# Small-K matmuls padded to 128 rows, and per-token factors spread by transposes of a repeated column

## The chip, the cores and the metric

The kernel runs on one core of a Trainium2 chip. The metric is the device time of one execution in microseconds, as the median of several runs; lower is better. A profile of one execution gives the rows that are quoted below. In it PE is TensorE (matmuls), PEld its weight loads, DVE VectorE, ACT ScalarE, POOL GpSimd and SP the engine that issues the transfers.

## The reference, cut to what matters

Two transformer blocks over 512 tokens of 1024 features, in float32. The first has neighbourhood attention (8 heads of 64 features, each query against 256 keys of its window and 256 context keys) beside a Hyena mixer with long convolutions, and a SwiGLU. The second has latent attention (8 heads of 96 features), a state-space branch, cross attention, and a convolutional feed-forward.

```python
def rmsnorm(x, g):
    y = xf * lax.rsqrt(jnp.mean(xf * xf, axis=-1, keepdims=True) + RMS_EPS)
...
    s_nb = jnp.einsum('brqhd,brikhd->bhrqik', grid(q_rot), k_band,
                      preferred_element_type=jnp.float32) * scale + bias[None]
    s_ctx = jnp.einsum('brqhd,bchd->bhrqc', grid(q), k_ctx, preferred_element_type=jnp.float32) * scale
    s = jnp.concatenate([s_nb.reshape(B, H, R, GRID_W, wh * GRID_W), s_ctx], axis=-1)
    p = jax.nn.softmax(s, axis=-1).astype(v.dtype)
...
    h = (hid @ w3.astype(f32)).reshape(L, 2, HY_ORDER, HY_WIDTH)
```

Three things of it matter here: the scores of the neighbourhood attention (a product over 64 features), the last product of the network that makes Hyena's filters (also over 64), and the factors that go with a token: one over the root mean square in every norm, and one over the softmax's sum in every attention.

## The kernel before, in words

Activations lie with features on the 128 partitions and tokens along the free axis. A float32 product is carried by three matmuls on 12-bit parts: a value is split into a high and a low part, and hi times hi, hi times lo and lo times hi are added in one bank of PSUM. A product over 64 features is packed into two matmuls: the queries' high and low parts stand on 64 partitions each and meet the keys' high parts, which stand there twice (128 rows); then the queries' high parts alone meet the keys' low parts, which takes 64 rows (`scores`, with the operands from `stacked_queries` and `stacked_keys`; the low parts of both heads share one tile). `filters` does the same with the filter network's hidden values. In `mla` the keys and queries of a head fill 96 rows.

A factor by token comes out of a sum with the tokens on the partitions, [128 tokens, n], and is needed along the free axis, the same on every partition. `to_rows` splits it into high and low parts (a copy on ACT, a subtraction on DVE), transposes both on PE into 2n rows, and copies them back to SBUF on ACT. Then `spread` (called by `bcast` for the norms) or `over_sums` (for the softmax's sums) makes each block of 128 tokens with a matmul of 4, 8 or 16 rows against a table of zeros and ones (`onehot`, `pick`).

The program is first traced into a list of calls. A planner (`Trace.schedule`, run forwards and backwards by `plan`) then orders the calls of each engine with a table of durations, hands out the memory (96 pages of 512 columns, 8 banks of PSUM), and `emit` issues them in the order of their planned starts. So every instruction of the profile has the line of `emit`, L690, and tiles are named after their pool: `pages` and `small` are SBUF, `banks` is PSUM. Each engine takes its instructions in that fixed order. Generators mix the work: the neighbourhood attention (two pairs of heads to a page, four query blocks to a head) is interleaved with Hyena's branch of the merge, the state-space branch with cross attention and the projections of the gates.

Of the kernel before, what the change touches and what calls it, by code (L numbers as in the profile page):

```python
"""Two transformer blocks on one core: a modulated block (neighbourhood attention beside a Hyena
mixer, SwiGLU) and a hybrid block (latent attention, S5, cross attention, convolutional GLU).

Activations lie with features on partitions and tokens on the free axis. A float32 product is
carried by three passes of 12-bit parts: x = hi + lo exactly, and hi*hi + hi*lo + lo*hi.
In the first block the tokens are ordered by column block, row, column within the block, so that
an attention window is a run of neighbouring tokens.
"""
# [16 lines left out]
P = 128  # L25
D = 1024
T = 512
# [5 lines left out]
SHARE = 0.5, 0.5  # of the memory kept back: for all else, for rounded operands  # L33
RESERVE = 4, 40, 0.05  # units kept back from calls ahead of others: at least, at most, by call
# [14 lines left out]
# columns of the packed per-feature vectors: name -> (first column, columns)  # L49
# [21 lines left out]
# ---------------------------------------------------------------- layout on the host  # L71
def _cols(v):
    """[n] -> [128, n/128], features on partitions (short vectors padded with zeros)."""
    v = np.asarray(v).reshape(-1)
    n = -(-v.size // P)
    w = np.zeros(n * P, v.dtype)
    w[: v.size] = v
    return w.reshape(n, P).T


def _blocks(w):
    """[K, M] -> groups of eight 128x128 blocks, ordered by output tile, then by input tile."""
    k, m = w.shape
    b = w.reshape(k // P, P, m // P, P).transpose(2, 0, 1, 3).reshape(-1, P, P)
    return np.ascontiguousarray(b.reshape(-1, 8, P, P).transpose(0, 2, 1, 3)).reshape(-1, P, 8 * P)


def _rows(w):
    """[1024, 512] -> groups of two input tiles, side by side"""
    return w.reshape(KT // 2, 2, P, T).transpose(0, 2, 1, 3).reshape(KT // 2, P, 2 * T)  # L90


def _token_perm():
    """perm[t'] = t for the token order of the first block."""
    t = np.arange(T)
    cb, r, c = t // 64, (t % 64) // 8, t % 8
    return r * 64 + cb * 8 + c


def _state_order():  # L100
    """the state-space branch's features by half of the group pairs, group of the pair, pair, channel"""
# [7 lines left out]
def _rpb_index():  # L109
    """Index into [na_rpb of a head | NEG] of every (query, key) of a window; three kinds of window."""  # L110
# [14 lines left out]
def _constants():  # L125
# [31 lines left out]
    c["onehot"] = np.repeat(np.eye(8, dtype=f), 2, 0)  # L157
    one = np.repeat(np.eye(8, dtype=f), 2, 0)
    c["pick"] = np.concatenate([np.repeat(one[:, :4], P, 1), np.repeat(np.stack([one[:, :4], one[:, 4:]], 2).reshape(16, 8), 64, 1)], 1)
# [5 lines left out]
def layout(inp):  # L165
# [4 lines left out]
    ones = lambda v: np.concatenate([v[:64], np.ones(32, v.dtype)])  # the rotated part has its gain in the tables  # L170
# [39 lines left out]
    # second block  # L210
# [17 lines left out]
    kvb = f1("w_kv_b_2").reshape(2, P, 2, 4, 2, 64)  # k, p, half, head, (key, value), dim  # L228
# [14 lines left out]
# ---------------------------------------------------------------- tracing  # L243
# The program is traced into a list of calls first. A list scheduler then orders the calls by the
# engines' rates and hands out the on-chip memory as pieces come and go, and they are emitted in that order.
ENGINES = ("tensor", "vector", "scalar", "gpsimd", "sync")
PE, DVE, ACT, POOL, DMA = range(5)
# ns from the end of a call to the start of one that waits for it, by their engines
# [7 lines left out]
ALONE = (DVE,)  # engines that urgent calls have to themselves  # L256
DMA_START = 1700.0
RELEASE = 200.0, 150.0, 150.0, 100.0, 1200.0
TABLES = {AF.Silu: (0,), AF.Sin: (1, 0), AF.Exp: (2,), AF.Gelu_apprx_tanh: (3,)}  # sets of functions of ACT
TABLE_LOAD = 1283.0  # L260
TICK, TICK_COLUMNS = 10240 / 3, 3060.0  # PE's clock is halved after a tick (ns) with fewer columns of 128 rows


class Piece:
    """a piece of an arena, or (arena None) memory that stays"""
# [7 lines left out]
    def box(self, ap):  # L273
        """the partitions and columns that a view may touch"""
# [14 lines left out]
    def access(self, number, box, write):  # L289
        """note an access; returns the calls that it must follow"""  # L290
# [11 lines left out]
class View:  # L302
    """an access pattern that knows its piece of memory"""
# [15 lines left out]
    def placed(self):  # L319
        """the access pattern where the piece has come to lie"""  # L320
# [16 lines left out]
class Arena:  # L337
    """memory in units of `unit` columns, in segments that each hold either rounded operands or
    anything else; the run of units that has been free for longest goes first"""
# [8 lines left out]
    def reset(self, counted):  # L348
        """for another schedule; `counted`: units are only counted"""
        self.counted = counted  # L350
        self.free = self.low = self.n
        self.room = [self.n, self.n]  # units for either kind
# [32 lines left out]
    def take(self, piece, ahead):  # L385
        """place a piece that goes `ahead` of the calls before it, if the memory left allows"""
# [62 lines left out]
class Engine:  # L449
    """an engine whose calls are traced"""  # L450
# [12 lines left out]
class Trace:  # L463
# [8 lines left out]
    def first(self):  # L472
        """calls that go before all others"""
# [5 lines left out]
    def time(engine, name, out, args, kw):  # L479
        """about how long a call holds its engine, in ns"""  # L480
# [17 lines left out]
    def may_swap(engines, name, kw):  # L498
        """whether either of DVE and GpSimd may take a call"""
# [38 lines left out]
    def schedule(self, order, back=False):  # L538
        """Start times and memory for all calls, by a list scheduler that goes by `order`; returns the time it
        takes. back: from the end to the start, on the engines chosen before."""  # L540
# [126 lines left out]
    def plan(self):  # L667
        """Schedules to and fro: each goes by the order that the one before it ended up with."""
# [24 lines left out]
# ---------------------------------------------------------------- the program  # L693
class Program:
# [16 lines left out]
    # tiles  # L711
# [13 lines left out]
    def pair(self, n=T):  # L725
        """a hi/lo pair [128, n]"""
# [8 lines left out]
    def kept(self, pool, shape, name):  # L735
        """memory that stays"""
# [16 lines left out]
    # hi/lo parts  # L753
    def lo(self, out, src, hi, pool=None):
        """out = src - hi"""
# [8 lines left out]
    def mm(self, out, w, x, start, stop):  # L764
        """out (+)= w^T x for hi/lo pairs"""
# [7 lines left out]
    def stream(self, ap):  # L773
        """the 128x128 blocks of a weight in order, as hi/lo pairs"""
# [8 lines left out]
    def proj(self, blocks, xs, n=T, tag="mm"):  # L783
        """one output tile: sum over the input tiles"""
# [5 lines left out]
    def proj_rows(self, ap, xs):  # L790
        """a projection to 512 features with the 256 tokens on partitions: two tiles in PSUM"""
# [45 lines left out]
    def when(self, name):  # L837
        """hold a filler until what it needs has been emitted"""
# [19 lines left out]
    def sincos(self, ang):  # L858
        """ang [parts, n], reduced in place; returns (sin, cos)"""
# [11 lines left out]
    def exp(self, x, n):  # L871
        """e^x for a few columns [128, n], to the last places; in place"""
# [1448 lines left out]
```

## Time and profile before

| | us |
|---|---|
| median of 3 runs | 1847.07 |
| lowest and highest of them | 1846.66 and 1848.56 |
| span of the profiled execution, from first to last instruction | 1843.7 |

The span is 3.4 us shorter than the median of the runs, which also hold what lies before the first and after the last instruction. The page of the profile has PE busy for 96% of the span, DVE for 66%, ACT for 40% and POOL for 20%. A matmul's record is longer than the step to the next one, since matmuls are pipelined; what a matmul costs PE is read from the length of a run of equal ones.

### The profile page before, as it was taken

The page shows a single profiled execution, that of the slowest core. Times are in us where ns is not written, and L with a number is a line of the kernel's source. Part 1 is how long each engine was busy: PE and PEld are TensorE (multiplying, and loading weights), DVE is VectorE, ACT ScalarE, POOL GpSimd, SP SyncE. Part 2 cuts the span into 40 slices and gives each one's busy share as a digit, 9 for nine tenths or more (in the row PEclk, how much of TensorE's full clock was granted, in tenths as well). Part 3 has the DMA queues.
Part 4 walks back from the last instruction along what each step waited for, and adds up shares of the span by engine and source line. Part 5 has one row for each costly group of instructions (what it writes and reads, how often), then busy time and mean ns, then how long its engine had stood idle before and what let it go on. Part 6 is the DMA issues. An engine that isn't in the chain of part 4 may idle for free. (4 is left out here: it accounts for less than half of the span.)

```text
span 1843.7 us, 23257 instructions
## 1 busy us (share of the span) xinstructions
PE 1768.5 (96%) x8523; PEld 1436.1 (78%) x8523; DVE 1216.2 (66%) x2254; ACT 737.3 (40%) x1259; POOL 362.1 (20%) x275
## 2 busy tenths in 40 slices
PE   5899989999989999999999999799999999999999
PEld 2478878777768887888888788588877888888887
DVE  7997885677799627544348654747997643897520
ACT  5543433565535412224325352345664321454320
POOL 6731321000244003211012100200223000031000
PEclk9899999999999999999999999899999999999999
DMA  6743232243676233433324463431148332221330
GB/s 229 233 144 109 82 109 91 98 142 115 215 260 239 101 129 126 126 91 106 124 78 159 165 174 98 124 132 59 47 143 268 120 108 71 92 69 60 129 125 18
DMA packets 93729, 235.51 MB, mean 128 GB/s; under 512 B 18364, under 2 KB 26300, under 8 KB 93614
## 3 DMA queue, kind: packets, MB, share of 16 engines
q1 hardware_dynamic: 93614, 234.02, 38.1%
q8 instruction: 67, 1.10, 0.2%
q14 instruction: 48, 0.39, 0.1%
HBM read 206.98 MB, written 27.00 MB: 127 GB/s over the span
## 5 line engine op out<-in xcount | busy, mean ns | idle before, releaser
L690 PE MATMUL banks<-pages,pages 128*128 128x512 f32 (+6 forms) x7833 | 1713.7, 376 | 53.6 <-DVE pages L690 42.8
L690 PEld LDWEIGHTS banks<-pages,pages 128*128 128x128 f32 (+4 forms) x7833 | 1358.9, 187 | 359.6 <-DVE pages L690 53.6
L690 DVE TENSOR_TENSOR pages<-pages,pages 128x1024 fp32r<-128x1024 f32 (+13 forms) x571 | 579.2, 1037 | 95.4 <-ACT pages L690 85.8
L690 POOL TENSOR_TENSOR pages<-pages,pages 128x512 f32<-128x512 f32 (+10 forms) x195 | 326.0, 1682 | 1091.3 <-ACT pages L690 660.9
L690 ACT CAST pages<-pages 128x1024 fp32r<-128x1024 f32 (+4 forms) x469 | 396.5, 872 | 358.8 <-DVE pages L690 107.5
L690 DVE TENSOR_TENSOR pages<-banks,pages 128x512 fp32r<-128x512 f32 (+7 forms) x219 | 112.0, 524 | 129.4 <-PE banks L690 99.0
L690 DVE TENSOR_TENSOR pages<-banks,R 128x512 f32<-128x512 f32 x81 | 57.0, 707 | 118.0 <-PE banks L690 117.7
L690 ACT ACTIVATE pages<-banks 128x512 f32<-128x512 f32 (+4 forms) x75 | 37.2, 512 | 211.6 <-PE banks L690 203.9
L690 DVE TENSOR_TENSOR pages<-pages,banks 128x512 f32<-128x512 f32 x66 | 44.0, 681 | 109.2 <-PE banks L690 100.5
L690 ACT ACTIVATE pages<-pages 128x512 f32<-128x512 f32 (+4 forms) x91 | 50.6, 570 | 145.8 <-DVE pages L690 145.3
L690 ACT COPY pages<-banks 128x512 f32<-128x512 f32 (+6 forms) x121 | 58.7, 502 | 99.2 <-PE banks L690 87.8
L690 DVE SCALAR_TENSOR_TENSOR pages<-pages,vec,pages 128x511 f32<-128x511 f32 (+3 forms) x120 | 94.7, 811 | 5.3 <-ACT pages L690 4.4
L690 ACT CAST pages<-banks 128x512 fp32r<-128x512 f32 (+8 forms) x147 | 60.9, 426 | 67.8 <-PE banks L690 63.9
L690 ACT ACTIVATE pages<-pages,vec 128x512 f32<-128x512 f32 (+1 forms) x84 | 63.2, 767 | 55.1 <-DVE pages L690 49.5
L690 PE MATMUL banks<-ident,pages 128*128 128x128 f32 (+3 forms) x461 | 73.7, 273 | 11.7 <-DVE pages L690 7.5
L690 PEld LDWEIGHTS banks<-ident,pages 128*128 128x128 f32 (+3 forms) x461 | 53.7, 139 | 26.1 <-DVE pages L690 9.4
L690 ACT ACTIVATE pages<-banks,small 128x512 f32<-128x512 f32 (+3 forms) x80 | 46.4, 587 | 21.8 <-DVE small L690 20.9
L690 POOL TENSOR_TENSOR pages<-pages 128x512 f32<-128x512 f32 (+5 forms) x18 | 20.7, 1153 | 118.7 <-DVE pages L690 106.8
L690 DVE SCALAR_TENSOR_TENSOR pages<-pages,pages 128x1024 bf16<-128x1024 f32 (+3 forms) x41 | 42.8, 1050 | 0.7 <-DMA bhy<-pages 0.5
L690 DVE SCALAR_TENSOR_TENSOR pages<-pages,banks 128x512 f32<-128x512 f32 x40 | 27.0, 679 | 12.6 <-PE banks L690 12.6
L690 DVE SCALAR_TENSOR_TENSOR pages<-banks,mod,pages 128x512 f32<-128x512 f32 x16 | 11.8, 747 | 34.7 <-PE banks L690 34.7
L690 DVE SCALAR_TENSOR_TENSOR small<-small 128x4 f32<-128x4 f32 (+2 forms) x150 | 31.9, 218 | 1.8
(81 smaller groups left out, 470.2 us busy)
## 6 DMA issues: line engine op xcount, KB each, us to landing
pages<-in_w_f_dram SPq DMA_DIRECT2D x66, 512.0 KB, 3.7
pages<-in_w_ada_dram SPq DMA_DIRECT2D x48, 512.0 KB, 6.5
pages<-in_w_up_dram SPq DMA_DIRECT2D x44, 512.0 KB, 3.3
pages<-in_w_g_dram SPq DMA_DIRECT2D x24, 512.0 KB, 3.8
pages<-in_w_down_dram SPq DMA_DIRECT2D x22, 512.0 KB, 3.6
pages<-in_w_out_dram SPq DMA_DIRECT2D x16, 512.0 KB, 6.6
pages<-in_w_hy_dram SPq DMA_DIRECT2D x12, 512.0 KB, 4.6
pages<-in_w_na_dram SPq DMA_DIRECT2D x12, 512.0 KB, 3.7
```

What stands on the lines that cost most here:

```text
L690: self.tc.keep_in_program_order(f(*map(at, c.args), **{k: at(v) for k, v in c.kw.items()}))
```

## The change

Every matmul of some size gets 128 rows. `stacked_keys` makes a tile of low parts for each head, with zeros (set on POOL) on the other head's 64 partitions, and `scores` uses all rows of the queries against it. `filters` makes a second pair of tiles, `hidz`, with the high parts on one half and zeros on the other. In `mla` the upper 32 partitions of queries and keys are set to zero and the scores' matmuls take all 128 rows.

`to_rows`, `spread` and the tables `onehot` and `pick` with their loads are gone. A column of factors, repeated 128 times by a step of zero, is transposed as it is: `bcast` and `over_sums` issue one transpose for each block of 128 tokens. For two heads a page, `over_sums` first copies the factors into a [128, 512] tile on DVE, 64 columns for each head.

The planner's rules and durations are the same; it plans anew.

```diff
-    def to_rows(self, r, n):
...
-    def spread(self, out, rows, j):
...
     def bcast(self, r, nb):
-        rows, ps = self.to_rows(r, nb), self.psum("t")
+        ps = self.psum("t")
         for b in range(nb):
-            self.spread(ps[:, b * P : b * P + P], rows, b)
+            self.transpose(ps[:, b * P : b * P + P], r[:, b : b + 1].to_broadcast([P, P]))
...
-            hidp = self.pair(256)
+            hidp, hidz = self.pair(256), self.pair(256)
...
+                nc.scalar.copy(hidz[hh][r], hid[r])
+                nc.gpsimd.memset(hidz[hh][o].bitcast(F32), 0.0)
...
-                    nc.tensor.matmul(ps, hidp[hh][rows, at], w[1][rows, cols], start=False, stop=True)
+                    nc.tensor.matmul(ps, hidz[hh][:, at], w[1][:, cols], start=False, stop=True)
...
-        rows, ps = self.to_rows(rec, n), self.psum("t")
+        ps = self.psum("t")
+        if n == 8:
+            wide = self.u2()
+            nc.vector.tensor_copy(wide.rearrange("p (b h d) -> p b h d", h=2, d=64), rec.rearrange("p (h b) -> p b h", b=4).unsqueeze(3).to_broadcast([P, 4, 2, 64]))
         for b in range(4):
-            nc.tensor.matmul(ps[:, b * P : b * P + P], self.pick[n // 8][: 2 * n, b * P : b * P + P], rows, start=True, stop=True)
-        self.pe += 224
+            self.transpose(ps[:, b * P : b * P + P], wide[:, b * P : b * P + P] if n == 8 else rec[:, b : b + 1].to_broadcast([P, P]))
...
-        hi, lo = [self.u2(n, F32R) for _ in range(2)], self.u2(n, F32R)
+        hi, lo = ([self.u2(n, F32R) for _ in range(2)] for _ in range(2))
...
-            self.lo(lo[r], x[r], hi[hd][r], pool=False)
+            self.lo(lo[hd][r], x[r], hi[hd][r], pool=False)
+            self.nc.gpsimd.memset(lo[hd][o].bitcast(F32), 0.0)
...
-        self.nc.tensor.matmul(out, q[hd][r, at], lo[r, off : off + 256], start=False, stop=True)
+        self.nc.tensor.matmul(out, q[hd][:, at], lo[hd][:, off : off + 256], start=False, stop=True)
...
+            for d in (*qd, *kd):
+                for t in d:
+                    nc.gpsimd.memset(t[96:].bitcast(F32), 0.0)
...
-                rows = lambda t, hd, c0, n: t[:96, hd * T + c0 : hd * T + c0 + n]
+                rows = lambda t, hd, c0, n: t[:, hd * T + c0 : hd * T + c0 + n]
```

The order of PE around the second spread of the norm between the two blocks (`final_norm`), before; `ident` marks a transpose, and a row names the bank and the two operands, with the size of the output:

```order
L690 MATMUL banks_65<-pages_4310,pages_5283 128x512
L690 MATMUL banks_65<-pages_3646,pages_5283 128x512
L690 MATMUL banks_65<-ident,pages_6526 8x128
L690 MATMUL banks_65<-pages_4310,pages_6240 128x512
L690 MATMUL banks_65<-pages_6473,pages_6308 128x512
L690 MATMUL banks_65<-pages_6479,pages_6308 128x512
L690 MATMUL banks_65<-pages_7454,onehot 128x128 x4
L690 MATMUL banks_65<-pages_6473,pages_7192 128x512
```

The same place of PE with the change:

```order
L687 MATMUL banks_65<-pages_6407,pages_5303 128x512
L687 MATMUL banks_65<-pages_6424,pages_5303 128x512
L687 MATMUL banks_65<-ident,small_64 128x128 x4
L687 MATMUL banks_65<-pages_6407,pages_6661 128x512
L687 MATMUL banks_65<-pages_6505,pages_2471 128x512
```

The transpose into 8 rows and, three matmuls later, the four small matmuls have become four transposes in one place, which read the factors straight from `small`.

The order of PE at the end of the first pair of heads of the neighbourhood attention, before (the transpose of this pair's factors, 16x128, stands 44 rows ahead):

```order
L690 MATMUL banks_65<-pages_164,pages_2087 128x512
L690 MATMUL banks_65<-pages_135,pages_1785 128x512
L690 MATMUL banks_65<-pages_726,pages_1785 128x512
L690 MATMUL banks_65<-pages_135,pages_2087 128x512
L690 MATMUL banks_65<-pages_1522,pick 128x128 x4
L690 MATMUL banks_65<-pages_187,pages_1785 128x512
```

With the change:

```order
L687 MATMUL banks_65<-pages_2606,pages_834 128x256
L687 MATMUL banks_65<-pages_2606,pages_1492 128x256
L687 MATMUL banks_65<-pages_432,pages_2471 128x512
L687 MATMUL banks_65<-ident,pages_2588 128x128 x4
L687 MATMUL banks_65<-pages_601,pages_2151 128x512
L687 MATMUL banks_65<-pages_693,pages_2151 128x512
```

The small matmuls are four transposes here too, of the copied tile; the matmuls around them are others, since the whole plan is new. The scores themselves stand in these lists as 128x256 before and after: the rows that they take from their operands aren't part of an output's size.

## Rows read from the trace of the kernel before

**Rows 1.** The page: span, PE's share, and PE's clock in 40 slices.

```profile
span 1843.7 us, 23257 instructions
...
PE 1768.5 (96%) x8523; PEld 1436.1 (78%) x8523; DVE 1216.2 (66%) x2254; ACT 737.3 (40%) x1259; POOL 362.1 (20%) x275
...
PEclk9899999999999999999999999899999999999999
```

**Rows 2.** Stretches: length, busy us (instructions) by engine, PE's clock, DMA, GB/s.

```profile
20.00:160.00 140.00, 124.43 (x514) 84.70 (x515) 129.90 (x176) 73.03 (x121) 73.83 (x39) 0.94 0.48 162
...
320.00:520.00 200.00, 199.42 (x974) 156.25 (x973) 142.90 (x307) 110.77 (x220) 25.01 (x17) 1.00 0.46 153
...
1000.00:1030.00 30.00, 25.63 (x114) 20.20 (x114) 25.92 (x78) 7.30 (x17) 12.16 (x13) 0.89 0.45 155
1160.00:1180.00 20.00, 10.15 (x49) 7.92 (x48) 15.03 (x11) 5.64 (x11) 8.59 (x5) 0.74 0.38 119
1180.00:1420.00 240.00, 236.22 (x1231) 195.88 (x1229) 181.51 (x517) 131.80 (x289) 42.70 (x34) 1.00 0.38 125
1440.00:1840.00 400.00, 400.00 (x1767) 330.25 (x1765) 214.16 (x264) 130.29 (x168) 32.42 (x19) 1.00 0.25 84
```

**Rows 3.** PE's instructions from 320 to 520 us, by form (rows*columns of weights, output).

```profile
L690 PE MATMUL banks<-pages,pages 128*128 128x512 f32 x554 | 146.8, 403 | 0.3 <-ACT pages L690 0.3
L690 PE MATMUL banks<-pages,pages 128*128 128x256 f32 x186 | 39.8, 302 | 0.0
L690 PE MATMUL banks<-ident,pages 128*128 128x128 f32 x156 | 23.8, 273 | 0.3 <-DVE pages L690 0.3
L690 PE MATMUL banks<-pages,pages 64*128 64x256 f32 x58 | 22.1, 381 | 0.0
```

**Rows 4.** Timeline of PE, four runs: start, length, first form, count.

```profile
384.64 0.60 PE L690 MATMUL banks<-ident,pages 128*128 128x128 f32 x4
...
388.72 1.01 PE L690 MATMUL banks<-pages,pages 64*128 64x256 f32 x3
...
597.73 2.52 PE L690 MATMUL banks<-pages,pages 128*128 128x256 f32 x19
...
1423.48 59.11 PE L690 MATMUL banks<-pages,pages 128*128 128x512 f32 x257 [3.26 <-DVE pages L690]
```

**Rows 5.** Timeline of PE at a softmax's factors, 513 to 516 us.

```profile
513.84 0.94 PE L690 MATMUL banks<-pages,pages 128*128 128x512 f32 x3
514.72 0.66 PE L690 MATMUL banks<-pages,pick 16*128 16x128 f32 x4
515.31 1.43 PE L690 MATMUL banks<-pages,pages 128*128 128x512 f32 x5
```

**Rows 6.** PE's instructions of the whole span by form: filters, and 384 columns.

```profile
L690 PE MATMUL banks<-pages,pages 128*128 128x384 f32 x72 | 15.3, 340 | 0.0
...
L690 PE MATMUL banks<-pages,pages 64*128 64x512 f32 x16 | 10.4, 647 | 0.0
...
L690 PE MATMUL banks<-pages,pages 96*128 96x384 f32 x24 | 6.2, 360 | 1.5 <-DVE small L690 0.9 <-DVE pages L690 0.6
```

**Rows 7.** Timeline of all engines at `final_norm`'s second spread.

```profile
1018.59 0.16 DVE L690 TENSOR_TENSOR small<-small 128x4 f32<-128x4 f32 x1
...
1018.78 0.20 ACT L690 CAST pages<-small 128x4 fp32r<-128x4 f32 x1 [5.75 <-DVE small L690]
...
1019.32 0.16 DVE L690 TENSOR_TENSOR pages<-small,pages 128x4 fp32r<-128x4 f32 x1
...
1019.54 0.38 PE L690 MATMUL banks<-ident,pages 128*8 128x128 f32 x1 [3.41 <-DVE pages L690]
...
1022.28 0.69 DVE L690 COPY R<-banks 128x512 f32<-128x512 f32 x1 [1.48 <-PE banks L690]
```

**Rows 8.** By form, whole span: a memset on POOL, a copy on DVE.

```profile
L690 POOL MEMSET pages<- 128x1024 f32 x5 | 4.8, 953 | 42.6 <-PE banks L690 33.6 <-DMA pages<-s5g 9.0
...
L690 DVE COPY pages<-pages 128x512 f32<-128x512 f32 x2 | 0.8, 422 | 0.0
```

More of the change, by code (lines that the diff above doesn't have):

```diff
@@ L156, in _constants @@
     c["cmask"] = np.where(np.arange(P)[None] <= np.arange(P)[:, None], 0.0, NEG).astype(f)
-    c["onehot"] = np.repeat(np.eye(8, dtype=f), 2, 0)
-    one = np.repeat(np.eye(8, dtype=f), 2, 0)
-    c["pick"] = np.concatenate([np.repeat(one[:, :4], P, 1), np.repeat(np.stack([one[:, :4], one[:, 4:]], 2).reshape(16, 8), 64, 1)], 1)
     c["eye16"] = np.tile(np.eye(16, dtype=f), (2, 1))
@@ L917, in rsqrt, with bcast @@
         return r
-    def to_rows(self, r, n):
-        nc = self.nc
-        t = self.pair(16)[0]
-        hi, lo = t[:, 0 : 2 * n : 2], t[:, 1 : 2 * n : 2]
-        nc.scalar.copy(hi, r)
-        self.lo(lo, r, hi, pool=False)
-        ps = self.psum("t")
-        self.transpose(ps[: 2 * n, :P], t.bitcast(F32)[:, : 2 * n])
-        rows = self.u2(P, F32R)[: 2 * n]
-        nc.scalar.copy(rows, ps[: 2 * n, :P])
-        return rows
-    def spread(self, out, rows, j):
-        k = rows.shape[0]
-        self.nc.tensor.matmul(out, self.onehot[:k, j : j + 1].to_broadcast([k, out.shape[0]]), rows, start=True, stop=True)
-        self.pe += 107
-    def bcast(self, r, nb):
-        rows, ps = self.to_rows(r, nb), self.psum("t")
+    def bcast(self, r, nb):
+        ps = self.psum("t")
         for b in range(nb):
-            self.spread(ps[:, b * P : b * P + P], rows, b)
+            self.transpose(ps[:, b * P : b * P + P], r[:, b : b + 1].to_broadcast([P, P]))
         return ps[:, : nb * P]
@@ L1017, in setup @@
         self.trace.add((POOL,), "identity", (self.ident,), {})
-        raw = self.u4(parts=16)
-        self.load(raw, a["pick"])
-        pick = self.const([P, 1024], name="pick").bitcast(F32R)[:16]
-        nc.scalar.copy(pick, raw)
-        self.pick = pick[:, :512], pick[:, 512:]
-        raw = self.u0(8, parts=16)
-        self.load(raw, a["onehot"])
-        self.onehot = self.const([P, 8], name="onehot").bitcast(F32R)[:16]
-        nc.scalar.copy(self.onehot, raw)
         self.ones = self.const([P, 2], name="ones")
@@ L1170, in filters @@
                     ps = self.psum()
-                    rows = slice(hh * 64, hh * 64 + 64)
                     w, cols, at = sd_w[j], slice(o * 512, o * 512 + 512), slice(p, p + 255, 2)
                     nc.tensor.matmul(ps, hidp[hh][:, at], w[0][:, cols], start=True, stop=False)
-                    nc.tensor.matmul(ps, hidp[hh][rows, at], w[1][rows, cols], start=False, stop=True)
+                    nc.tensor.matmul(ps, hidz[hh][:, at], w[1][:, cols], start=False, stop=True)
                     self.pe += 430
@@ L1434, in stacked_keys @@
             self.nc.scalar.copy(hi[hd][o], x[r])
-            self.lo(lo[r], x[r], hi[hd][r], pool=False)
+            self.lo(lo[hd][r], x[r], hi[hd][r], pool=False)
+            self.nc.gpsimd.memset(lo[hd][o].bitcast(F32), 0.0)
         return hi, lo
     def scores(self, out, hd, q, at, k, off):
-        r, (hi, lo) = slice(hd * 64, hd * 64 + 64), k
+        hi, lo = k
         self.nc.tensor.matmul(out, q[hd][:, at], hi[hd][:, off : off + 256], start=True, stop=False)
-        self.nc.tensor.matmul(out, q[hd][r, at], lo[r, off : off + 256], start=False, stop=True)
+        self.nc.tensor.matmul(out, q[hd][:, at], lo[hd][:, off : off + 256], start=False, stop=True)
         self.pe += 218
```

## Prediction

> **What bounds the kernel now.** I looked at the page first: PE is busy for 1768.5 of 1843.7 us, and its clock is at or near the full level in almost every slice [rows 1]. So PE is the bound of the whole, but its share says neither whether its time is spent well nor whether each stage hangs on it. The stretches answer the second question [rows 2]. From 320 to 520 us, where the neighbourhood attention runs, PE is busy for 199.4 of 200 us at clock 1.00 while DVE has 142.9 us of work: PE alone sets the pace. From 1440 us on it is 400.0 of 400; the change touches almost nothing there. From 20 to 160 us DVE has 129.9 of 140 us and PE waits for it: what PE saves there is worth little. At 1000 to 1030 and 1160 to 1180 us PE waits in its fixed order and then runs at half clock (means 0.89 and 0.74).
>
> The first question needs the price of one matmul, which a record does not give; a run of equal ones does [rows 4]. 257 matmuls of 512 columns take 59.11 us; less the last one's record of 0.403 [rows 3] that is 0.229 us a step. In the same way 256 columns cost (2.52 - 0.302) / 18 = 0.123, and a 128x128 transpose (0.60 - 0.273) / 3 = 0.109. The run at 388.72 us is the scores' 64 rows, 128 rows, 64 rows, all of 256 columns: (1.01 - 0.381) / 2 = 0.314 us a step, for columns that cost 0.123 elsewhere. Both steps are long, into the 64-row matmul and out of it.
>
> As a check, I summed the stretch from 320 to 520 us by these steps [rows 3]: 554 x 0.229 + 244 x 0.123 (58 with 64 rows among them) + 156 x 0.109 = 173.9 us, and some 2.8 us for the 20 small matmuls and transposes of the factors. PE was busy for 199.4. The 22.7 us left over fall on the 58, 0.39 us each, and twice 0.314 - 0.123 is 0.38. The two agree, and this is what the prediction rests on.
>
> The Trainium skill, "TensorEngine Tiling (Array Packing)", Key Properties, says that changing the tiling mode drains TensorE, and it counts 64 rows as another mode than 128; the row agrees. "TensorE: Matmul & The Clock Gate" of the Trainium skill, Why this matters for your kernels, says that a single matmul of 32 rows takes as long as one of 128 rows. By that sentence zeros beside the low parts would bring nothing, and it is the first rival below; the row speaks against it where 64 and 128 rows alternate.
>
> **The change, part by part.** *Scores.* 64 matmuls of 64 rows (4 pages, 2 heads, 4 blocks, 2 each) lose 0.39 us: 25 us of PE's time. How much comes through depends on what is late next, which is DVE: 142.9 us of work would stand in 175 instead of 200, 82%. Where DVE has 76% (1180 to 1420), PE is busy for 98.4%; where it has 93% (20 to 160), for 89% [rows 2]. On a line between these, 82% costs PE some 5%, 9 us; but the DVE-rich end is the start of the program, where data is still missing, so I take half, 4 us. **-21**, with -25 and -16 as ends.
>
> *Factors.* 29 times (17 spreads for norms, 12 softmax sums) a group of two or four small matmuls becomes as many transposes. At 514.72 us [rows 5] the last 512-column matmul begins at 513.84 + 0.94 - 0.403 = 514.38, so the step to the first small one is 0.34 instead of 0.229; four small ones then take 0.59 to the next start, where four transposes take 4 x 0.109 = 0.44. That is 0.26 us a group. The transpose into rows goes too, whose step I put at 0.03 (it begins almost with its neighbour). 29 x 0.27 = 8 us at most, less the groups where PE waits anyway and the six that have two blocks: **-6**, ends 0 and -8.
>
> *The chain of a factor.* At `final_norm` the factors are done at 1018.75, ACT copies, DVE subtracts at 1019.32, PE transposes at 1019.54 after 3.41 us of idling, and R is copied only at 1022.28 [rows 7]. With the change PE can go on some 0.6 us earlier, and R is there after four transposes instead of a transpose, a copy, and four small matmuls: about 2 us of 3.5, in a place where PE's banks wait for R. There are two such spreads and the first norm's; elsewhere other work covers the chain. **-3**, ends 0 and -6.
>
> *Filters.* 16 matmuls of 64 rows have records of 647 ns on the mean against 403 [rows 3, 6]; with the step before each I estimate 2 x 0.24 x 16 = 8 us of PE. They lie in the stretch where DVE has 93%. **-1**, ends 0 and -8.
>
> *Latent attention.* With 96 rows, 384 columns have a record of 360 ns against 340 with 128 rows [rows 6], and waits are in it. 96 such matmuls of four sizes make at most 96 x 0.02 = 2 us. I take 0: 96 rows seem to cost what 128 do.
>
> *Added work.* 34 memsets on POOL, none dearer than the 953 ns of a full 1024-column one [rows 8]: at most 32 us on an engine that works for 20% of the span [rows 1]. If a matmul of the latent attention had to wait for the eight that its half needs, that would be 8 x 0.95 = 8 us; projections of the gates cover it. **0**, ends 0 and +8. On DVE eight copies of 512 columns at 0.42 [rows 8] replace 29 subtractions at 0.16 [rows 7], 3.4 against 4.6 us: nothing. ACT loses 58 short copies, SP two loads; neither was waited for long.
>
> *The order.* The planner plans anew, and its durations for the scores, which left the 0.39 out, now fit better. Stalls can come and go: the dearest one, at 1160 to 1180 us, costs 9.85 us of idling and 20 x 0.26 = 5.2 us of clock [rows 2]. I add **+2**, ends -8 and +8.
>
> Sum: -21 - 6 - 3 - 1 + 0 + 2 = **-29 us**. In the profile the span would go from 1843.7 to about 1815; the runs, 3.4 us above it, from 1847.1 to **1818 us**.
>
> **Rivals.** (1) *Rows don't matter.* The long step could belong to something that stays, such as two matmuls that add into one bank. Then only the chain and the dropped transposes count: -3 - 1 = -4, 1843 us. Against it: every projection adds into one bank at 0.229 a step. 4%. The sentence of the Trainium skill's "TensorE: Matmul & The Clock Gate" given above is this rival's.
>
> (2) *DVE takes over in the neighbourhood attention.* The scores bring 12 instead of 21: -20, 1827 us. For it: DVE has 93% and more in other stretches; against it: 142.9 us still fit well into 175. 14%.
>
> (3) *More comes through.* The whole 25, the 8 of the factors, the 8 of the filters, and a stall less: -42, 1805 us. 12%.
>
> (4) *One new stall of the size of that at 1160 us*, about 15 us: 1833 us. 5%.
>
> (5) *Slower: the clock falls at the transposes.* 104 of them replace matmuls, in 29 places. If PE's clock fell at each as it does around 1020 us, a place would cost 30 x 0.11 = 3.3 us [rows 2]. From ten places on this eats the gain; at fifteen it is +50 - 31, 1866 us. Against it: from 320 to 520 us 156 transposes stand between matmuls and the granted clock is 1.00 throughout [rows 2, 3], and the new ones come in groups of 0.4 us. 3%. The Trainium skill, "TensorE: Matmul & The Clock Gate", Part 4: PE-mode transpose, says that transposes don't count as busy for the clock; the stretch named here shows no loss by it when matmuls surround them.
>
> **How the numbers follow.** The forecast itself has 62%, with a range of its own from 1808 to 1826 us. Taking in rivals 2 and 4 above and most of 3 below, the range is 1803 to 1837 us; it leaves out rivals 1 and 5 and the tail of 3. A measurement of this kernel tells 0.2%, 3.7 us, from no change. Faster by more than that: all of the forecast and rivals 2, 3 and 4, and half of rival 1, less a little for stalls that add up, 0.93. Within: the rest of rival 1, 0.03. Slower: rival 5 and several stalls together, 0.04.
>
> **What would show it.** No form with 64 rows is left on PE, and the step in a run of scores is 0.12 us. The stretch of the neighbourhood attention, the 200 us here, becomes some 21 us shorter with DVE's share near 80%; if PE's share falls below 95% there, rival 2 is right. Runs of four transposes take 0.6 us in place of the small matmuls' 0.66, and the steps around them are not longer. The clock's mean is 0.98 or above; below it, rival 5 gets weight. After 1440 us nothing changes but the stretch's place. The prediction is wrong if the scores' runs keep their 0.31 us, or if PE idles in new places for more than 20 us.

## The result, and the profile after

The changed kernel takes 1801.02 us (median of 4 runs, 1798.32 to 1804.63) against 1847.82 (4 runs): a ratio of 0.9754, interval 0.9736 to 0.9772, 46.8 us less. The forecast was 1818 us with a range from 1803: the sign and the mechanism were right, and the gain was more than half as large again as the 29 us of the sum, 2 us beyond the range's lower end. The profiled execution of the changed kernel is the longest of its four, 1804.63 us; in the profiles the span goes from 1843.7 [rows 1] to 1802.8 us.

The page after, the lines that answer to [rows 1]:

```profile
span 1802.8 us, 23185 instructions
...
PE 1720.8 (95%) x8494; PEld 1423.4 (79%) x8494; DVE 1219.3 (68%) x2245; ACT 724.4 (40%) x1199; POOL 363.2 (20%) x297
...
PEclk9899999999989999999999999999999999999999
```

PE's busy time falls from 1768.5 to 1720.8, by 47.7 us, with only 29 instructions fewer. What the span has beyond it grows from 75.2 to 82.0 us. So the gain is PE's own time, shorter steps, and waiting gives back some 7 us of it. DVE, ACT and POOL have about the work that they had.

The stretches after that answer to [rows 2] (length, busy us and instructions by engine, PE's clock, DMA, GB/s); the neighbourhood attention now lies from 300 to 470 us, the dear stall at 1124, the end from 1400 on:

```profile
20.00:160.00 140.00, 120.43 (x567) 87.69 (x568) 132.70 (x184) 75.88 (x121) 72.20 (x42) 0.94 0.49 166
300.00:470.00 170.00, 165.58 (x905) 140.70 (x904) 139.89 (x300) 102.58 (x201) 44.00 (x31) 0.99 0.47 163
...
1124.00:1144.00 20.00, 12.32 (x67) 10.24 (x66) 18.60 (x18) 6.97 (x12) 8.16 (x5) 0.83 0.35 107
1144.00:1380.00 236.00, 222.97 (x1166) 187.31 (x1165) 182.56 (x495) 125.64 (x275) 58.76 (x45) 0.99 0.36 126
1400.00:1800.00 400.00, 399.10 (x1761) 329.14 (x1759) 214.10 (x265) 130.18 (x166) 26.98 (x17) 1.00 0.24 83
```

In the neighbourhood attention PE is busy for 97% where it was for 100, and DVE has 82% where it had 71: DVE comes closer, but does not take over. The last 400 us are as before. PE's forms in the same stretch (form, count, busy us, mean ns of a record), for [rows 3]:

```profile
L687 PE MATMUL banks<-pages,pages 128*128 128x512 f32 x514 | 133.2, 400 | 2.7 <-DVE pages L687 2.7
L687 PE MATMUL banks<-pages,pages 128*128 128x256 f32 x235 | 35.6, 286 | 1.4 <-DVE pages L687 1.4
L687 PE MATMUL banks<-ident,pages 128*128 128x128 f32 x156 | 23.3, 273 | 0.3 <-ACT pages L687 0.3
```

The form of 64 rows is gone, and the 256-column records are shorter by 16 ns on the mean. Of the chain of a factor, the place of [rows 7] in the timeline of all engines:

```profile
978.98 0.15 DVE L687 TENSOR_TENSOR small<-small 128x4 f32<-128x4 f32 x1
...
979.60 0.60 PE L687 MATMUL banks<-ident,small 128*128 128x128 f32 x4
...
980.24 0.69 DVE L687 COPY R<-banks 128x512 f32<-128x512 f32 x1 [1.11 <-PE banks L687]
```

The factors are done at 979.13 and R is copied from 980.24 on, 1.1 us later instead of 3.5, and PE has no idle time ahead of the transposes. PE's waits in the whole span (us in all, times, longest):

```profile
PE banks L687 <- DVE pages L687: 52.3, 28, 8.9
PE banks L687 <- ACT pages L687: 13.1, 7, 8.1
PE banks L687 <- DVE small L687: 9.1, 4, 5.2
PE banks L687 <- DMA pages<-in_hy_mlp_dram: 3.4, 1, 3.4
PE banks L687 <- POOL pages L687: 0.3, 1, 0.3
```

POOL's new memsets are waited for at most 0.3 us. "DVE small" is the factors: transposes now wait for them directly, once for 5.2 us.

### The profile page after: what moved, and what is told of

Its sections match the earlier page's. It is cut to its first block, busy times and chain, and to the rows that moved or that the text cites. A ratio compares the mean times of both kernels' runs of the same rounds, so it can differ in the third digit from the quotient of the medians.

```text
span 1802.8 us, 23185 instructions
## 1 busy us (share of the span) xinstructions
PE 1720.8 (95%) x8494; PEld 1423.4 (79%) x8494; DVE 1219.3 (68%) x2245; ACT 724.4 (40%) x1199; POOL 363.2 (20%) x297
## 4 chain that ended last, share of the span: by engine, by line
PE 81%; DVE 10%; DMA 2%; issue 2%; ACT 1%; SPq 0%; POOL 0%; DVEq 0%; POOLq 0%; ACTq 0%
PE banks L687 81%; DVE pages L687 8%; DVE small L687 1%; DMA pages<-in_w_out_dram 1%; ACT pages L687 1%; SPq L687 0%; DMA pages<-in_w_xq_dram 0%; DMA pages<-in_w_mem_dram 0%; DVE banks L687 0%; DMA pages<-s5g 0%; DMA pages<-in_w_ada_dram 0%; POOL pages L687 0%; DMA ud<-pages 0%; DVE gs L687 0%; DVE mod L687 0%
## 5 line engine op out<-in xcount | busy, mean ns | idle before, releaser
L687 PE MATMUL banks<-pages,pages 128*128 128x512 f32 (+6 forms) x7835 | 1676.5, 373 | 58.5 <-DVE pages L687 46.0
L687 PEld LDWEIGHTS banks<-pages,pages 128*128 128x128 f32 (+3 forms) x7835 | 1350.1, 186 | 335.6 <-DVE pages L687 57.5
L687 DVE TENSOR_TENSOR pages<-pages,pages 128x1024 fp32r<-128x1024 f32 (+12 forms) x574 | 572.5, 1020 | 114.2 <-ACT pages L687 102.7
L687 ACT CAST pages<-pages 128x1024 fp32r<-128x1024 f32 (+5 forms) x471 | 398.3, 871 | 399.2 <-DVE pages L687 93.8
L687 POOL TENSOR_TENSOR pages<-pages,pages 128x512 fp32r<-128x512 f32 (+11 forms) x187 | 306.9, 1650 | 939.8 <-ACT pages L687 538.2
L687 DVE TENSOR_TENSOR pages<-banks,pages 128x512 fp32r<-128x512 f32 (+8 forms) x219 | 111.4, 522 | 117.0 <-PE banks L687 91.5
L687 PE MATMUL banks<-ident,pages 128*128 128x128 f32 (+2 forms) x464 | 72.5, 276 | 7.2 <-DVE pages L687 5.7
L687 PEld LDWEIGHTS banks<-ident,pages 128*128 128x128 f32 (+2 forms) x464 | 56.5, 145 | 22.5 <-issue 5.6
L687 ACT CAST pages<-banks 128x512 fp32r<-128x512 f32 (+5 forms) x118 | 53.2, 469 | 37.5 <-PE banks L687 26.6
L687 DVE SCALAR_TENSOR_TENSOR pages<-pages,pages 128x1024 bf16<-128x1024 f32 (+2 forms) x39 | 52.8, 1367 | 0.1
```

The costliest lines, as they stand in the source:

```text
L687: self.tc.keep_in_program_order(f(*map(at, c.args), **{k: at(v) for k, v in c.kw.items()}))
```

## The experiments

All kernels that ran stand in one table. "At full clock" is the span of the profiled execution times its mean granted clock: how long it would be had PE's clock been at its upper level, 2.4 GHz, throughout. That takes a little too much off, since the clock is also low while PE waits (of the 58 us that the kernel before spends at 1.2 GHz, PE is busy in 47), but it helps to compare executions with different clocks. A last digit of the clock is 1.8 us. The product is good to some 5 us only: the four executions of e11 have spans from 1805.6 to 1809.7 us with clocks from 0.983 to 0.988, and products from 1775 to 1787. The ratio is the one on record; the quotient of the medians differs from it by up to 0.001.

| kernel | median us | ratio to before (interval) | span | clock | at full clock |
|---|---|---|---|---|---|
| before | 1847.8 | 1 | 1843.7 | 0.984 | 1814.2 |
| changed | 1801.0 | 0.9754 (0.9736 to 0.9772) | 1802.8 | 0.984 | 1774.0 |
| e1 scores with 64 rows | 1822.3 | 0.9866 (0.9848 to 0.9885) | 1821.4 | 0.988 | 1799.5 |
| e2 filters with 64 rows | 1804.2 | 0.9766 (0.9747 to 0.9785) | 1800.8 | 0.989 | 1781.0 |
| e3 scores, short rows paired | 1812.5 | 0.9809 (0.9793 to 0.9825) | 1812.5 | 0.984 | 1783.5 |
| e4 latent attention, 96 rows | 1802.0 | 0.9750 (0.9732 to 0.9767) | 1800.2 | 0.984 | 1771.4 |
| e5 changed, old factors | 1814.3 | 0.9818 (0.9803 to 0.9832) | 1813.5 | 0.989 | 1793.6 |
| e6 before, new factors | 1816.3 | 0.9836 (0.9817 to 0.9854) | 1813.1 | 0.990 | 1795.0 |
| e7 changed, window 900 | 1796.1 | 0.9722 (0.9707 to 0.9736) | 1795.3 | 0.986 | 1770.2 |
| e8 before, window 900 | 1851.4 | 1.0014 (1.0001 to 1.0027) | 1850.7 | 0.980 | 1813.7 |
| e9 as e6, window 900 | 1822.1 | 0.9855 (0.9840 to 0.9870) | 1819.9 | 0.986 | 1794.4 |
| e10 as e5, window 900 | 1803.9 | 0.9757 (0.9742 to 0.9772) | 1801.4 | 0.987 | 1778.0 |
| e11 changed, longer chain | 1809.5 | 0.9786 (0.9769 to 0.9804) | 1806.1 | 0.983 | 1775.4 |
| e12 as e11, short rows | 1822.9 | 0.9854 (0.9838 to 0.9871) | 1817.9 | 0.983 | 1787.0 |
| e13 before, true durations | 1848.9 | 0.9998 (0.9986 to 1.0011) | 1846.5 | 0.985 | 1818.8 |
| e14 as e13, window 900 | 1855.1 | 1.0040 (1.0026 to 1.0054) | 1849.8 | 0.985 | 1822.0 |
| e15 as e6, true durations | 1825.9 | 0.9877 (0.9856 to 0.9898) | 1827.3 | 0.985 | 1799.9 |

**Rows put back on the changed kernel's own order (e1 to e4).** The planner plans with 128 rows, so that order and memory are those of the changed kernel; when the calls are emitted, the two operands are cut to the short rows:

```
+            if c.rows is not None:
+                c.args = (c.args[0], c.args[1][c.rows], c.args[2][c.rows])
```

`rows` is set around the second matmul of `scores` (e1: 64 rows), that of the filters (e2: 64 rows), or the latent attention's score matmuls (e4: 96 rows). e3 is e1 with the two middle matmuls of two neighbouring scores exchanged, so that the 64-row ones stand in pairs: 128, 128, 64, 64.

> The changed kernel with its plan, order and memory as they are; only the scores' matmuls with the keys' low parts take 64 rows again instead of 128 (the zeros are set, but not used). Theory A (a step into or out of a 64-row matmul costs PE 0.19 us more, and PE sets the pace there): 64 matmuls x 0.39 = 25 us, so about 1826 us against the changed kernel's 1801, and the runs of scores show 0.31 us a step. Theory B (DVE takes over a part, as the prediction had it): 16 to 21 us more, 1817 to 1822. Theory C (the new plan brought the gain): within 5 us of 1801.

> The changed kernel with its plan as it is; only the 16 matmuls of the filters' last product take 64 rows again. Theory A (PE's steps count there too): 8 to 11 us more than 1801, so 1809 to 1812. Theory B (DVE sets the pace of the first 100 us, as the prediction had it): 0 to 2 us more.

> As the run with 64-row scores, but where the four matmuls of two scores stand together on PE, the two of 128 rows go first and the two of 64 rows follow. Theory D (what costs is the change between 64 and 128 rows): a group of four has two changes instead of four, so about half of the extra, 12 to 14 us over 1801, and the step between the two 64-row matmuls is near 0.12 us. Theory E (a 64-row matmul is slow in itself, as is the one behind it): the same extra as ungrouped, some 25 us, and that step is 0.31 us.

> The changed kernel with its plan as it is; only the latent attention's 96 score matmuls take 96 rows again instead of 128. All theories: within 3 us of 1801 (a record of 96 rows took 360 ns against 340 of 128, waits included, 2 us in all); if 96 rows cost a change as 64 do, 96 x 0.19 or more, 18 us.

Measured: 21.3 us more for e1, 3.2 for e2, 11.5 for e3, 1.0 for e4; the intervals of e2 and e4 overlap with that of the changed kernel. The median of e1 is at the upper end of theory B, though its steps are those of theory A; e2 is nearest to its theory B, e3 just below the 12 of theory D. The same 13 matmuls (eight of scores with 256 columns, among which five with 512) in the timeline of PE, first in the changed kernel, then in e1, then in e3:

```profile
372.26 2.35 PE L687 MATMUL banks<-pages,pages 128*128 128x256 f32 x13
```

```profile
378.26 3.92 PE L689 MATMUL banks<-pages,pages 128*128 128x256 f32 x13
```

```profile
374.71 3.13 PE L696 MATMUL banks<-pages,pages 128*128 128x256 f32 x13
```

Four short matmuls cost 1.57 us when each stands alone, 0.39 each, and 0.78 when they stand in pairs. So what costs is the change of the row mode, twice for each lone matmul and twice for each pair, and not the short matmul itself. The step between the two short matmuls of a pair, for which D had 0.12 and E 0.31 us, is 0.22: a change lengthens the step that leads to it by 0.09 and the one behind by 0.10, and the second of these falls between the two. A group of 96 rows shows no such price: in e4 the steps around these matmuls, where PE neither waits nor runs at 1.2 GHz, are 0.07 us longer in all. In spans at full clock e1 is 25.5 us above the changed kernel, the whole of 64 x 0.39; by the medians 21.3 come through. Matched matmul by matmul, PE loses 24.7 us at the 64 short matmuls of e1, none of it in a wait.

**Factors and orders apart, planned anew (e5 to e10).** e5 is the changed kernel with `to_rows`, `spread`, the one-hot tables and `over_sums` of before; e6 is before with the new `bcast` and `over_sums`. In e7 to e10 the same four corners are planned with one number changed, which gives every engine another order:

```
-WINDOW = 1000
+WINDOW = 900
```

> The changed kernel with the factors spread in the old way (split into rows, one transpose, a copy, small matmuls by the one-hot tables); scores, filters and latent attention keep their 128 rows, and the planner plans anew. The experiments so far account for 24.5 us of the 46.8 (scores 21.3, filters 3.2, latent attention 0). Theory F (the remaining 22 us are the factors': shorter steps and a shorter chain at each of the 29): this kernel loses them, about 1823 us, within 5 of it. Theory O (the factors are worth the forecast 9 or less, the rest is the luck of the new order of the instructions): 1810 us if this plan is as lucky as that of the changed kernel; another plan may fall anywhere from 1805 to 1830, so that F and O are told apart only together with the three other kernels of this group.

> The kernel before with the new way of spreading the factors alone; scores, filters and latent attention keep their short rows, and the planner plans anew. Theory F: 22 us less than before, about 1826 us, within 5. Theory O: 9 less or not even that, 1838 to 1848 us.

> The changed kernel with one number of the planner changed (the window of calls ahead, 900 in place of 1000): the same instructions in another order. It measures what an order is worth. Theory F: within 5 us of 1801, since orders differ little. Theory O: the order of the changed kernel is a lucky one by some 10 us or more, so another is slower: 1808 to 1820 us.

> The kernel before with the same number of the planner changed (900 in place of 1000). Theory F: within 5 us of 1848. Theory O: the order of before may be an unlucky one; another is faster by some 10 us, 1830 to 1840.

> The kernel before with the new way of spreading the factors alone, as the earlier run of that edit, but with the planner's window at 900. With the three other kernels of this window it gives the price of the factors and of the long rows a second time, in other orders. Against the kernel before at 900 (1851.35): theory S (the factors are worth the PE steps that they save, about 12 us, and the rest of the 32 us of the earlier run was the luck of its order): 1835 to 1843 us. Theory L (the shorter chain of a factor is worth another 10 or more in any order): 1819 to 1832 us.

> The changed kernel with the factors spread in the old way, with the planner's window at 900. Against the changed kernel at 900 (1796.1): theory S 1806 to 1811 us, theory L 1813 us or more.

The new factors alone bring 32 us (e6) and 29 (e9 against e8), far more than any term had allowed; beside full rows they bring 13 (e5) and 8 (e10 against e7). F holds for e7 and e8 alone, which stay within 5 us; e5 lies between O and F, and e6 brings more than F. L holds for e9, and e10 lies below even S. At full clock the first four corners become plain: 1814.2 before, 1795.0 with the new factors, 1793.6 with the full rows, 1774.0 with both. The factors are worth 19.2 and 19.6 us there, the rows 20.6 and 21.0: in the profiled executions the parts add up, and the 18 us by which they seem to disturb each other in the medians go with the clock, 0.990 and 0.989 in e6 and e5 against 0.984 in the kernel before and in the changed one. Over all executions of the four kernels the mean products give 21 and 17 us for the factors, so that the parts add up to some 4 us. At the window of 900 the factors are worth 19.3 us beside short rows and 7.8 beside full rows; that gap of 11 the clock does not explain.

The profiles show where it lies. PE's work, that is its busy time less half of what falls into stretches at 1.2 GHz, is 1745.2 us before and 1726.8 in e6, 1713.8 in e5 and 1696.6 in the changed kernel; at the window of 900 it is 1738.4 in e8 and 1723.9 in e9, 1710.7 in e10 and 1696.9 in e7. So the new factors save 18.4 and 17.2, then 14.5 and 13.8 us of PE's work, about as much beside short rows as beside full ones. What differs is PE's idle time, the span less the busy time: the new factors shorten it by 3.7 and 2.4 us, and at the window of 900 they shorten it by 8.4 beside short rows and lengthen it by 6.0 beside full rows. What an order does to the waits of a factor can be read in e8. PE's timeline there, at the transpose into rows of the norm ahead of the second block's memory:

```profile
552.76 2.88 PE L690 MATMUL banks<-pages,pages 128*128 128x512 f32 x12
568.30 0.37 PE L690 MATMUL banks<-ident,pages 128*4 128x128 f32 x1 [12.66 <-DVE pages L690]
```

PE idles for 12.66 us at one transpose of the old chain; in the order of the kernel before it idles for 0.2 us there. DVE's timeline shows what the factor waits for:

```profile
556.53 0.15 DVE L690 TENSOR_TENSOR small<-small 128x2 f32<-128x2 f32 x1
556.60 1.21 DVE L690 SCALAR_TENSOR_TENSOR pages<-pages,pages 128x1024 bf16<-128x1024 f32 x1
...
557.74 0.15 DVE L690 SCALAR_TENSOR_TENSOR small<-small 128x2 f32<-128x2 f32 x1
...
568.09 0.15 DVE L690 TENSOR_TENSOR pages<-small,pages 128x2 fp32r<-128x2 f32 x1
```

Between two of the factor's small operations stands one of 1.21 us that has nothing to do with it, down to the subtraction at 568.09 on which the transpose waits: most steps of the chain on DVE take 1.2 us instead of 0.15. The new way drops one such step, and the changed kernel, whose order mixes the same two chains, still waits at this norm:

```profile
530.49 0.69 PE L687 MATMUL banks<-ident,small 128*128 128x128 f32 x2 [5.22 <-DVE small L687]
```

The same norm in e9, in e10 and in e7:

```profile
553.14 0.43 PE L687 MATMUL banks<-ident,small 128*128 128x128 f32 x2 [0.99 <-DVE small L687]
```

```profile
530.04 0.27 PE L690 MATMUL banks<-ident,pages 128*4 128x128 f32 x1 [1.83 <-DVE pages L690]
```

```profile
523.99 0.43 PE L687 MATMUL banks<-ident,small 128*128 128x128 f32 x2 [4.24 <-DVE small L687]
```

From e8 to e9 the new factors shorten this one wait by 11.7 us, from e10 to e7 they lengthen it by 2.4. That is 14.1 of the 14.4 us by which the idle times part, so that in these profiles the gap at the window of 900 is the waiting at one norm, and not another price of the factors.

**The factor's chain and its steps, on the changed kernel's order (e11, e12).** Behind the last operation of each factor three copies onto itself are emitted; in e12 the third goes to a rounded tile, and the transposes become matmuls with 4 to 16 rows at the same places:

```
+            if c.tag and c.tag[0] == "factor":
+                r = at(c.tag[1])
+                for copy in (self.nc.scalar.copy, self.nc.vector.tensor_copy, self.nc.scalar.copy):
+                    self.tc.keep_in_program_order(copy(r, r))
```

```
+            if c.tag and c.tag[0] == "spread":
+                x, b = small[id(c.tag[1].piece)], c.tag[2]
+                self.tc.keep_in_program_order(self.nc.tensor.matmul(at(c.args[0]), x[:, b : b + 1].to_broadcast([x.shape[0], P]), one[: x.shape[0]], start=True, stop=True))
+                continue
```

> The changed kernel with the order and the memory that it has, and behind the last operation of each factor (before it is spread) three copies of the factor onto itself, on ACT, DVE and ACT: the chain gets as long as the old one, and PE's instructions are the same. Theory L (the chain's length counts): each of the 29 waits some 0.6 us longer and much of it shows, 1811 us or more. Theory S (other work covers the chain at most places): 1801 to 1806 us.

> As the run with the longer chain, and the four (or two) transposes of each factor are matmuls of 4 to 16 rows again, at the same places; their results are not the factors, so that the values of the normalised tensors are wrong and only the time is of use. Against the run with the longer chain: both theories 0.26 us at each of 29 places less the two-block ones, 6 to 9 us more; if the short matmuls' row mode costs nothing between transposes and matmuls, 0.

Measured: the longer chain costs 8.5 us by the medians, 5.9 by the ratios to before, and 3.3 by the spans of the profiles, since the changed kernel's profiled execution was a long one. That lies between S and L: part of the chain shows. In the profiles PE's idle time is 82.5 us against 82.0, so that what is lost at some factors is found again elsewhere. One place where the chain shows is the first norm; e11's timeline there (small is the factor; the copies are on L691):

```profile
81.40 0.15 DVE L687 SCALAR_TENSOR_TENSOR small<-small 128x4 f32<-128x4 f32 x1
...
81.59 0.19 ACT L691 COPY small<-small 128x4 f32<-128x4 f32 x1 [0.93 <-DVE small L687]
81.81 1.97 DVE L691 COPY small<-small 128x4 f32<-128x4 f32 x1 [0.26 <-ACT small L691]
83.82 0.19 ACT L691 COPY small<-small 128x4 f32<-128x4 f32 x1 [2.04 <-DVE small L691]
...
84.07 1.11 PE L687 MATMUL banks<-ident,small 128*128 128x128 f32 x4 [3.44 <-ACT small L691]
```

The short rows (e12) cost another 13.4 us by the medians and 11.8 by the spans of the profiled executions, which have the same clock, 0.983; 6 to 9 were expected. The other executions went at 0.984 to 0.988 in e11 and at 0.978 and 0.979 in e12, so that the medians may hold some clock as well. A group in PE's timeline, first e11 with four transposes, then e12 with four matmuls of 16 rows, between the same neighbours:

```profile
390.38 0.86 PE L687 MATMUL banks<-pages,pages 128*128 128x512 f32 x3
391.08 0.60 PE L687 MATMUL banks<-ident,pages 128*128 128x128 f32 x4
391.43 1.41 PE L687 MATMUL banks<-pages,pages 128*128 128x512 f32 x5
```

```profile
392.07 0.86 PE L694 MATMUL banks<-pages,pages 128*128 128x512 f32 x3
392.86 0.66 PE L691 MATMUL banks<-one,narrow 16*128 16x128 f32 x4
393.45 1.43 PE L694 MATMUL banks<-pages,pages 128*128 128x512 f32 x5
```

From the first start to that of the third row it is 1.05 us with transposes and 1.38 with short rows, and the run behind is 0.02 longer: 0.35 us a group. Matched matmul by matmul, the 29 places make 11.4 us of the difference between the two profiles; 3.4 of them lie where PE waits or runs at 1.2 GHz. Elsewhere a place costs 0.3 to 0.35 us as a rule, and 0.13 to 0.20 in five.

**Whether the planner's durations are to blame (e13 to e15).** Its time of a matmul knows columns alone; here it is told the price of short rows, with no other change to the program:

```
-                return max(n / 2.4 + 2.5, cols / 1.2)
+                rows = args[1].shape[0]
+                return max(n / 2.4 + 2.5, cols / 1.2) + (380 if rows == 64 else 90 if rows <= 16 else 0)
```

> The kernel before with the same instructions, and the planner told what short rows cost: 380 ns more for each matmul of 64 rows and 90 ns more for each of 16 rows or fewer. The planner makes another order. The factors were worth 32 and 29 us beside short rows and 13 and 8 us beside full rows. Theory M (the planner's wrong durations for short rows spoil its order, so that waits of the old chain show that it believes covered; the full rows cure that too): 1828 to 1838 us, some 10 to 20 less than before. Theory N (the difference is the scatter of orders and has no such cause): 1843 to 1853 us.

> The same with the planner's window at 900, where the kernel before stands at 1851.35. Theory M: 1830 to 1841 us. Theory N: 1846 to 1856 us.

> The kernel before with the new way of spreading the factors alone (1816.34 us), and the planner told the same durations. Theory M: no better than without them, since this kernel has no old chain whose waits could show, 1812 to 1821 us. If the durations help here as much as in the two runs of the kernel before, the old chain isn't what they spoil.

Measured: 1848.9 and 1855.1 us, no better than before, and e15 is 9.6 us worse than e6. Theory M falls. In spans the two are 14.2 us apart, at full clock 4.9, so that the larger part is the clock. The orders of one program that ran here differ by up to some 10 us, and truer durations didn't make them better.

## Why the forecast was right in kind and wrong in size

**What bounds the kernel, and the mechanism: right.** PE's share, the stretch at 100% and the step of 0.314 us pointed to the change of the row mode. Experiments e1 and e3 show it: the short rows cost 21.3 us, and about half as many changes cost 11.5. The rule of the Trainium skill, "TensorEngine Tiling (Array Packing)", Key Properties, that a change of the tiling mode drains TensorE agrees with 2.35, 3.13 and 3.92 us. The sentence of the Trainium skill's "TensorE: Matmul & The Clock Gate", Why this matters for your kernels, that a single matmul of 32 rows takes as long as one of 128, is no guide where 64 and 128 rows alternate (0.314 against 0.123 us a step).

**Scores, -21: right in size, by luck.** 21.3 measured. The discount from 25 was argued with DVE, and DVE's share of 82% did not produce it: from 300 to 530 us e1 falls behind by 24.1 us of the 24.7. What its span lacks of that lies elsewhere and goes with the clock, 0.988 against 0.984.

**Factors, -6 with ends 0 and -8: the step that failed.** The short rows of the groups alone measured 11.8 us in two profiles of the same clock and 13.4 by the medians (e12 against e11), beyond the term's end, before the transpose into rows is counted. The working shows why. "That is 0.26 us a group" compared four small matmuls up to the next start with four transposes of 0.109, and left out the 512-column matmul that follows. With 128 rows the four transposes take 0.35 to the next start and lengthen the step behind by 0.09, where the prediction's signs had it no longer; the small ones take 0.59 and lengthen it by 0.11, and the step ahead by 0.09: 0.35 us a group. The forecast's own price from the scores, 0.19 us for a change of rows, would have given 0.38 for a group that is entered once and left once. The same omission sits in "whose step I put at 0.03": behind that transpose the first row of [rows 5] has (0.94 - 0.403) / 2 = 0.269 us a step instead of 0.229, 0.08 more over two steps, so 0.11 each. In the trace of the kernel before, 14 such transposes stand between 512-column matmuls without a wait and at 2.4 GHz, and each costs 0.11 to 0.12 us; 29 x 0.11 = 3.2 us is an estimate from that. Both together are some 29 x 0.46 = 13.3 us where the forecast had 8; "less the groups where PE waits anyway" then took 2 off that the runs do not bear out. The four pairs of kernels that were planned anew put the factors at 14 to 18 us of PE's work.

**The chain, -3 with ends 0 and -6: not settled.** Three copies more cost 3.3 us by the spans of the profiles, within the ends, and 8.5 by the medians, beyond them (e11). With the old chain planned in, e5 and e10 lose 13 and 8 us on the whole, and the steps alone are 13, so that a planner can hide that chain almost entirely in some orders; in others, as in e8, PE waits for 12.66 us at a single factor.

**Filters, -1: not refuted.** 3.2 us (e2), with intervals that overlap. PE's work is 6.2 us longer in e2, near the 8 that were estimated. But the profiled e2 is 1.1 us behind at 76 us, after the last of these matmuls, and no longer behind at 120 us; by then it has spent 6.8 us at 1.2 GHz and the changed kernel 17.1. So anything from nothing to some 6 us came through, and part of the 7.0 at full clock is the clock's.

**Latent attention 0 and added work 0: right** (e4; 0.3 us of waiting for POOL). **Order, +2 with ends -8 and +8:** right in size. The parts on the changed kernel's own order are 21.3 + 3.2 + 13.4 + 8.5 + 3.2 = 49.6 us against 46.8, which leaves +3 for the rest, with an uncertainty of several us since five differences are added; e7 and e8 moved by -5 and +3, e13 to e15 by up to 10. The profiles say it in fewer terms: PE's work falls by 48.6 us, where the forecast had counted 25 + 8 + 8 = 41 and let 28 of them through, and its idle time grows by 7 where the forecast had 1 less.

**Rivals.** Nearest to what came is rival 3, "more comes through", at -42, and some 5 us more; it had 12%, and the range's lower end cut its tail. Of its conditions, the whole price of the scores' and the factors' steps came; the whole of the filters' isn't shown, and no stall went, since idle time grew by 7 us. Rival 1 falls with e1; rival 2 with 97% of PE in the stretch; rival 4 with the total, though the changed kernel has new waits (5.22 us above); rival 5 with a mean clock of 0.984 in both kernels.

**Open.** That one wait makes the gap at the window of 900 was read from the traces and not varied: no run keeps one order in all four corners, and why PE's work falls by 18 and 17 us in one window and by 14 in the other isn't known. Nor was the clock's part in a run's time varied by itself; it was read beside the spans alone.

## What to carry to other kernels

Price an edit on a saturated engine by the whole run, from the start of the matmul ahead to the second start behind, since a change of form lengthens its neighbours' steps as well as its own. Where an engine is busy for 97 to 100% of a stretch, take the whole of what its steps lose and let the discounts widen the range instead of moving its middle; here 24.1 of 24.7 us came through in such a stretch, with DVE at 82%. For the filters' stretch, where DVE has 93%, the runs don't tell. And before two planned versions are called additive or not, multiply their spans by their granted clocks, and part the engine's work from its idle time: 0.984 against 0.990 is 11 us of 1840, and one wait was 12.66, more than most of the parts that were to be told apart.

## What the runs showed that was not expected

Matmuls with 64 rows in pairs cost half as much as alone (11.5 against 21.3 us), so that where zeros beside the low parts can't be had, an order that groups the short rows has half the gain. For 96 rows among 128 no price shows (1802.0 against 1801.0 us). The mean granted clock of one and the same order was 0.984 in the profiled executions of the changed kernel, e3 and e4, and 0.988 and 0.989 in those of e1 and e2, some 8 us of span by the product above; the four executions of the changed kernel alone went from 0.984 to 0.988. Among the profiled orders it went from 0.980 to 0.990. The fastest kernel of all is the changed one at the window of 900: 1796.1 us, ratio 0.9722 (0.9707 to 0.9736), though no edit but the order's number stands behind its 5 us.
